# Issuing each bulk load of a row-sum kernel as two 64-partition DMAs from two queues

## The chip, the cores and the metric

The kernel runs on one core of one Trainium2 chip. The metric is the device time in microseconds (us) of one execution; medians of several runs are quoted, and lower is better. With one core, "slow" only marks a run that is over 1.5% above the fastest of the same kernel.

## The reference

The reference sums rows of 1024 numbers and divides by 1024. The input is 32 x 512 = 16384 rows, 67.1 MB in all; the output is 64 KB.

```python
def reference(x, divisor):           # x: (32, 512, 1024) float32, divisor = 1024.0
    return (np.sum(x, axis=-1) / divisor).astype(np.float32)
```

Every byte is read once, and there is next to nothing to compute. The kernel can be no faster than its loads.

## The kernel before

The 16384 rows are laid out as 128 partitions x 128 rows, so each partition owns 512 KB of consecutive memory. The loads take 8 rows of every partition at a time (4.19 MB in one DMA), all from SyncE's queue, into five tile buffers. VectorE sums five of the eight rows, ScalarE the other three.

```python
    bulk = [8] * 15
    tail = [4, 2, 1]
    pool = ctx.enter_context(tc.tile_pool(name="bulk", bufs=5))
    ...
    def sums(t, j, rows, for_act):
        d = rows - for_act
        if d:
            nc.vector.reduce_sum(out=res[:, j : j + d], in_=t[:, :d, :], axis=AX)
        for r in range(d, rows):
            act_sum(res[:, j + r : j + r + 1], t[:, r, :])

    j = 0
    for rows in bulk:
        t = pool.tile([P, 8, D], F32, name="t")
        nc.sync.dma_start(out=t[:, :rows, :], in_=xr[:, j : j + rows, :])
        sums(t, j, rows, rows * 3 // 8)
        j += rows
    ...  # loads of 4, 2 and 1 rows, and a last row in three pieces, all 128 partitions wide
```

## Time and profile before

| | before |
|---|---|
| median time | 164.75 us |
| load queues | one, 96.5% of the 16 DMA engines' span |
| rate of the loads, 40 to 120 us | 433 GB/s |
| one row of a load (32 KB in one partition) | 1.213 us, 27.0 GB/s per DMA engine |
| VectorE, ScalarE busy | 53%, 36% |

The rows of the loads are the DMA packets that the trace records, each with its size and duration; the profile page counts 3169 packets. 16 engines at 27.0 GB/s are 432 GB/s, which is the measured rate. The durations of rows were read from these records; no line of a page shows a single row. The records do not say which engine carried a row, so what the expectations below say of single engines is the author's picture and not a reading.

Three lines of the page of the kernel before. The first two cut the span into 40 slices (busy share of the DMA engines in tenths, then GB/s); the third is the load queue with its packets, MB and share of the 16 engines' time.

```profile
DMA  6999999999999999999999999999999999999990
GB/s 209 426 418 443 435 435 435 418 443 435 410 459 426 402 467 435 394 459 435 426 443 418 435 437 418 443 435 410 443 443 402 459 443 410 443 435 398 408 352 16
q1 hardware_dynamic: 3168, 67.18, 96.5%
```

The same kernel's stretches: the columns are the stretch, its length, busy time of VectorE, ScalarE and GpSimd (with instruction counts), clock, DMA share and GB/s.

```profile
40.00:80.00 40.00, 21.95 (x4) 13.79 (x24) 0.00 (x0) 1.00 1.01 433
80.00:120.00 40.00, 21.95 (x4) 13.78 (x24) 0.00 (x0) 1.00 1.01 433
```

The DMA engines do not pause from the second slice to the last landing at 158.7 us, and the two compute engines have slack. So whatever a change does to the rate of the loads, or to keeping their queue filled, shows in full in the time; what it does to the sums matters only after the last load has landed.

### The profile page before, as it was taken

To read this page: it belongs to the slowest core of one execution; us is meant where nothing else is said; L and a number is where in the kernel's file an instruction comes from. 1 tells how busy PE (TensorE), PEld (TensorE's weight loads), DVE (VectorE), ACT (ScalarE), POOL (GpSimd) and SP (SyncE) were. 2 spreads that over 40 slices of the span, in tenths; PEclk is the share of its full clock that TensorE was granted. 3 is DMA by queue.
4 is the path that set the end of the run, shared out by engine and by line. 5 is a ranking of instruction groups with operands and counts; after the bars stand their busy time and mean duration, and the time that the engine had idled before them with its cause. 6 is when DMAs were issued, how large, how long until landed. Compare 5 with 4: busy or idle time off the path is not lost.

```text
span 162.9 us, 222 instructions
## 1 busy us (share of the span) xinstructions
DVE 87.1 (53%) x22; ACT 58.1 (36%) x101; POOL 0.2 (0%) x4
## 2 busy tenths in 40 slices
DVE  0007639094571917549093672908448092763983
ACT  3006135080531607034080622608043070613692
POOL 0000000000000000000000000000000000000000
DMA  6999999999999999999999999999999999999990
GB/s 209 426 418 443 435 435 435 418 443 435 410 459 426 402 467 435 394 459 435 426 443 418 435 437 418 443 435 410 443 443 402 459 443 410 443 435 398 408 352 16
DMA packets 3169, 67.18 MB, mean 412 GB/s; under 512 B 352, under 2 KB 736, under 8 KB 992
## 3 DMA queue, kind: packets, MB, share of 16 engines
q1 hardware_dynamic: 3168, 67.18, 96.5%
q14 instruction: 1, 0.01, 0.0%
HBM read 67.11 MB, written 0.07 MB: 412 GB/s over the span
## 4 chain that ended last, share of the span: by engine, by line
DMA 90%; DVE 7%; issue 1%; SPq 0%; DVEq 0%
DMA t<-in_x_dram 61%; DMA last<-in_x_dram 30%; DVE res L53 7%; DVE part L77 0%; DVE res L76 0%; DVE part L78 0%; DVE res L79 0%; SPq L60 0%; DVE part L74 0%; DVEq L78 0%
## 5 line engine op out<-in xcount | busy, mean ns | idle before, releaser
L53 DVE TENSOR_REDUCE res<-t 128x5 f32<-128x5120 f32 x15 | 82.3, 5488 | 72.5 <-DMA t<-in_x_dram 72.5
L48 ACT ACTIVATE junk<-t 128x1024 f32<-128x1024 f32 x45 | 46.2, 1027 | 99.2 <-DMA t<-in_x_dram 98.3
L48 ACT ACTIVATION_READ_ACCUMULATOR junk<-t 128x1 f32 x45 | 8.4, 186 | 0.0
L48 ACT ACTIVATE junk<-tail 128x1024 f32<-128x1024 f32 x4 | 4.1, 1028 | 1.7 <-DMA tail<-in_x_dram 1.7
L53 DVE TENSOR_REDUCE res<-tail 128x2 f32<-128x2048 f32 (+1 forms) x2 | 3.4, 1743 | 0.0
L48 ACT ACT_TABLE_LOAD x1 | 1.3, 1283 | 0.7 <-PEq L97 0.7
L74 DVE TENSOR_REDUCE part<-last 128x1 f32<-128x512 f32 x1 | 0.7, 685 | 0.6 <-DMA last<-in_x_dram 0.6
L48 ACT ACTIVATION_READ_ACCUMULATOR junk<-tail 128x1 f32 x4 | 0.7, 186 | 0.0
L77 DVE TENSOR_REDUCE part<-last 128x1 f32<-128x256 f32 x1 | 0.4, 411 | 0.0
L48 ACT ACTIVATE junk<-last 128x256 f32<-128x256 f32 x1 | 0.4, 388 | 0.0
L76 DVE TENSOR_SCALAR res<-res 128x127 f32<-128x127 f32 x1 | 0.2, 216 | 0.0
L78 DVE TENSOR_REDUCE part<-part 128x1 f32<-128x3 f32 x1 | 0.2, 155 | 0.1
L48 ACT ACTIVATION_READ_ACCUMULATOR junk<-last 128x1 f32 x1 | 0.2, 187 | 0.0
L79 DVE TENSOR_SCALAR res<-part 128x1 f32<-128x1 f32 x1 | 0.2, 154 | 0.0
L97 POOL MEMSET const-uint8-127<- 128x1 uint8 x1 | 0.1, 102 | 0.0
L97 POOL MEMSET const-bfloat16-1.0<- 128x1 bf16 x1 | 0.1, 101 | 0.0
L97 POOL MEMSET const-float32-0.0<- 128x1 f32 x1 | 0.1, 98 | 0.2 <-issue 0.2
L97 POOL MEMSET const-float32-1.0<- 128x1 f32 x1 | 0.1, 98 | 0.0
## 6 DMA issues: line engine op xcount, KB each, us to landing
t<-in_x_dram SPq DMA_DIRECT2D x15, 4096.0 KB, 43.0
tail<-in_x_dram SPq DMA_DIRECT2D x1, 2048.0 KB, 47.5
tail<-in_x_dram SPq DMA_DIRECT2D x1, 1024.0 KB, 49.5
tail<-in_x_dram SPq DMA_DIRECT2D x1, 512.0 KB, 50.4
last<-in_x_dram SPq DMA_DIRECT2D x1, 256.0 KB, 48.2
last<-in_x_dram SPq DMA_DIRECT2D x2, 128.0 KB, 34.1
out_dram<-res SPq DMA_DIRECT2D x1, 64.0 KB, 1.5
```

The lines of the kernel that those rows point to most:

```text
L48: nc.scalar.activation(junk[:, :n], src, COPY, accum_out=dst)
L53: nc.vector.reduce_sum(out=res[:, j : j + d], in_=t[:, :d, :], axis=AX)
L74: nc.vector.reduce_sum(out=part[:, 0:1], in_=last[:, 0:h], axis=AX)
L76: nc.vector.tensor_scalar_mul(out=res[:, :j], in0=res[:, :j], scalar1=scale)
L77: nc.vector.reduce_sum(out=part[:, 2:3], in_=last[:, h + q : D], axis=AX)
L78: nc.vector.reduce_sum(out=part[:, 3:4], in_=part[:, 0:3], axis=AX)
L79: nc.vector.tensor_scalar_mul(out=res[:, j : j + 1], in0=part[:, 3:4], scalar1=scale)
L97: nc = _bacc.Bacc("TRN2", target_bir_lowering=False, num_devices=1)
```

## The change

The intent: fewer, larger loads (14 rows instead of 8), the last rows shared between VectorE and ScalarE, and each bulk load issued as two DMAs of 64 partitions, one from SyncE's queue and one from ScalarE's. The core of the diff:

```diff
-    bulk = [8] * 15
-    tail = [4, 2, 1]
-    assert sum(bulk) + sum(tail) + 1 == J
-    pool = ctx.enter_context(tc.tile_pool(name="bulk", bufs=5))
+    bulk = [14] * 8 + [8]
+    split = {14: 6, 8: 4, 4: 2, 2: 1}
+    tail = [4, 2]
+    assert sum(bulk) + sum(tail) + 2 == J
+    pool = ctx.enter_context(tc.tile_pool(name="bulk", bufs=3))
...  (four junk tiles instead of one for ScalarE's sums; ScalarE's sums stand first)
-    for rows in bulk:
-        t = pool.tile([P, 8, D], F32, name="t")
-        nc.sync.dma_start(out=t[:, :rows, :], in_=xr[:, j : j + rows, :])
-        sums(t, j, rows, rows * 3 // 8)
+    for i, rows in enumerate(bulk):
+        t = pool.tile([P, 14, D], F32, name="t")
+        for q, a in ((nc.sync, 0), (nc.scalar, P // 2)):
+            tc.keep_in_program_order(q.dma_start(out=t[a : a + P // 2, :rows, :], in_=xr[a : a + P // 2, j : j + rows, :]))
+        sums(t, j, rows)
         j += rows
...  (the last two rows are split between the engines at column 704)
```

More of the change, by code (lines that the diff above doesn't have):

```diff
@@ L33 @@
     out_v = out.tensor.reshape((P, J)).ap()
-    bulk = [8] * 15
-    tail = [4, 2, 1]
-    assert sum(bulk) + sum(tail) + 1 == J
-    pool = ctx.enter_context(tc.tile_pool(name="bulk", bufs=5))
+    bulk = [14] * 8 + [8]
[3 more added lines that the diff above has]
+    pool = ctx.enter_context(tc.tile_pool(name="bulk", bufs=3))
     one = ctx.enter_context(tc.tile_pool(name="one", bufs=1))
-    psum = ctx.enter_context(tc.tile_pool(name="junk", bufs=1, space=bass.MemoryType.PSUM))
+    psum = ctx.enter_context(tc.tile_pool(name="junk", bufs=4, space=bass.MemoryType.PSUM))
@@ L42, with sums @@
     res = one.tile([P, J], F32, name="res")
     part = one.tile([P, 4], F32, name="part")
-    junk = psum.tile([P, D], F32, name="junk")
     def act_sum(dst, src):
         n = src.shape[-1]
+        junk = psum.tile([P, D], F32, name="junk")
         nc.scalar.activation(junk[:, :n], src, COPY, accum_out=dst)
-    def sums(t, j, rows, for_act):
-        d = rows - for_act
-        if d:
-            nc.vector.reduce_sum(out=res[:, j : j + d], in_=t[:, :d, :], axis=AX)
+    def sums(t, j, rows):
+        d = rows - split[rows]
@@ L54, in sums @@
         for r in range(d, rows):
             act_sum(res[:, j + r : j + r + 1], t[:, r, :])
+        nc.vector.reduce_sum(out=res[:, j : j + d], in_=t[:, :d, :], axis=AX)
     j = 0
-    for rows in bulk:
-        t = pool.tile([P, 8, D], F32, name="t")
-        nc.sync.dma_start(out=t[:, :rows, :], in_=xr[:, j : j + rows, :])
-        sums(t, j, rows, rows * 3 // 8)
+    for i, rows in enumerate(bulk):
[3 more added lines that the diff above has]
+        sums(t, j, rows)
@@ L62 @@
         j += rows
-    for k, rows in enumerate(tail):
-        t = one.tile([P, rows, D], F32, name=f"tail{k}")
-        nc.sync.dma_start(out=t, in_=xr[:, j : j + rows, :])
-        sums(t, j, rows, (rows + 1) // 2)
+    for i, rows in enumerate(tail):
+        t = one.tile([P, rows, D], F32, name=f"tail{i}")
+        tc.keep_in_program_order(nc.sync.dma_start(out=t, in_=xr[:, j : j + rows, :]))
+        sums(t, j, rows)
         j += rows
-    h, q = D // 2, D // 4
-    last = one.tile([P, D], F32, name="last")
@@ L72 @@
-    for a, b in ((0, h), (h, h + q), (h + q, D)):
-        nc.sync.dma_start(out=last[:, a:b], in_=xr[:, j, a:b])
-    nc.vector.reduce_sum(out=part[:, 0:1], in_=last[:, 0:h], axis=AX)
-    act_sum(part[:, 1:2], last[:, h : h + q])
-    nc.vector.tensor_scalar_mul(out=res[:, :j], in0=res[:, :j], scalar1=scale)
-    nc.vector.reduce_sum(out=part[:, 2:3], in_=last[:, h + q : D], axis=AX)
-    nc.vector.reduce_sum(out=part[:, 3:4], in_=part[:, 0:3], axis=AX)
-    nc.vector.tensor_scalar_mul(out=res[:, j : j + 1], in0=part[:, 3:4], scalar1=scale)
@@ L80 @@
-    nc.sync.dma_start(out=out_v, in_=res)
+    c = 704
+    t = one.tile([P, D], F32, name="row")
+    tc.keep_in_program_order(nc.sync.dma_start(out=t, in_=xr[:, j, :]))
+    act_sum(part[:, 0:1], t[:, c:])
+    nc.vector.reduce_sum(out=part[:, 1:2], in_=t[:, :c], axis=AX)
+    nc.vector.tensor_scalar(
+        out=res[:, j : j + 1], in0=part[:, 1:2], scalar1=part[:, 0:1], scalar2=scale, op0=ADD, op1=MULT
+    )
+    nc.vector.tensor_scalar_mul(out=res[:, :j], in0=res[:, :j], scalar1=scale)
+    j += 1
@@ new lines @@
+    t = one.tile([P, D], F32, name="last")
+    tc.keep_in_program_order(nc.sync.dma_start(out=t[:, :c], in_=xr[:, j, :c]))
+    tc.keep_in_program_order(nc.sync.dma_start(out=t[:, c:], in_=xr[:, j, c:]))
+    act_sum(part[:, 2:3], t[:, :c])
+    nc.vector.reduce_sum(out=part[:, 3:4], in_=t[:, c:], axis=AX)
+    nc.vector.tensor_scalar(
+        out=res[:, j : j + 1], in0=part[:, 3:4], scalar1=part[:, 2:3], scalar2=scale, op0=ADD, op1=MULT
+    )
+    tc.keep_in_program_order(nc.sync.dma_start(out=out_v, in_=res))
```

## The prediction

> What bounds the kernel now: the loads. The page gives the one load queue 96.5% of the 16 engines' span and 412 GB/s on average; the stretches from 10 to 150 us show 429 to 433 GB/s. VectorE is busy 53%, ScalarE 36%. The chain of waits is 90% DMA; only about 2 us of compute follow the last landing (158.7 us). All loads are issued by SyncE, which does nothing else, with up to five 8-row tiles ahead, so the queue never runs dry.
>
> What the change moves. Every bulk load becomes two 64-partition halves. SyncE's halves still run ahead, three tiles deep. ScalarE's half sits in ScalarE's program: its instruction order is half of load 0, table load and six row sums of load 0, then half of load 1, six sums, half of load 2, and so on. So ScalarE's half of load k+1 starts only after load k has landed and ScalarE has summed it; only one is ever in flight. Two costs follow.
>
> 1. A serial chain per 14-row load: landing, six sums at 1.18 us (start to start in the timeline: 13.38, 14.56, 15.74), 7.1 us; issue and start[...], about 2 to 3 us (the first load took 12.63 us where 4.19 MB at 433 GB/s are 9.7 us); then the transfer of the half, 3.67 MB. VectorE's 8-row sum, 8.8 us (5.49 us for five rows), then frees the buffer for SyncE's half of load k+3, so SyncE too is held back after the first loads and its half runs beside ScalarE's, not in the gap.
>
> 2. The rate. [...]Nothing in the trace of before shows a half-width load. If the two queues overlap perfectly, a half takes 17 us (3.67 MB at half of 433) and the chain's period is about 26 us[...].
>
> Summing nine loads by such a model: about 238 us with perfect overlap[...].[...]
>
> Smaller terms: the table load (1.28 us) now waits for ScalarE's first half; SyncE's queue has no work at the end, so the last two ScalarE halves run alone; VectorE's order has the tail and last-row sums before loads 7 and 8, which costs little because ScalarE ends last. The gain meant (fewer loads, shared last rows) is under 2 us and is lost, since the last rows land long before the end.
>
> Predicted: 300 us, 8 in 10 between 225 and 345. Faster by over 2%: 1%; within 2%: 1%; slower: 98%.
>
> What would show it: two load queues on the page; GB/s in the slices falling to 200 to 300 with regular dips to about 0 to 220 while ScalarE sums; ScalarE's half issued right after the sixth sum of the load before; the chain of waits alternating ScalarE sums and DMA; SyncE waiting for buffers (for VectorE or ScalarE).[...] VectorE's and ScalarE's sums should cost the same per row.
>
> What would make it wrong: half-width loads at full rate (then about 218 us); ScalarE's issues running ahead of its sums, so that the rate alone counts (165 us with perfect overlap)[...].

The sum over nine loads had three branches: about 238 us with perfect overlap (30%), 270 to 295 us between (25%), and 336 us if the two queues' transfers did not overlap, which it called "serialized" (40%). The 300 us lie between them. Only the 238 us can be followed from the trace of the kernel before: nine loads of about 26 us each, the author's estimate from six sums at 1.18 us, 2 to 3 us of issue and start, and 17 us for 3.67 MB at half of 433 GB/s.

## The result, and the profile after

The changed kernel took 334.39 us in the median (332.5 to 335.47), against 164.75 us. The ratio is 2.03, with a 95% interval of 2.02 to 2.04. Ratios here are the mean time of one kernel's fast runs over that of the other's of the same rounds, so not quite the ratio of the medians.

The same lines of the page of the changed kernel; q1 is SyncE's queue, q10 ScalarE's.

```profile
DMA  9999989999999989899999898999999899979900
GB/s 221 221 221 214 193 165 200 221 221 221 221 221 221 221 186 186 179 221 221 221 221 221 186 221 165 201 221 221 221 221 221 173 189 260 270 156 315 198 0 8
q1 hardware_dynamic: 1584, 35.72, 49.3%
q10 hardware_dynamic: 720, 31.46, 45.0%
```

Two of the changed kernel's stretches, with the columns as before:

```profile
56.00:86.00 30.00, 0.00 (x0) 0.00 (x0) 0.00 (x0) 1.00 1.02 214
98.00:110.00 12.00, 0.00 (x0) 0.00 (x0) 0.00 (x0) 1.00 1.03 220
```

The DMA engines are as busy as before (94.3% for both queues together), but they move half as much (202 GB/s on average by the page, against 412): busy engines are not fast engines. The trace's packet records say it directly. A row of a bulk load is now 56 KB, and its median duration is 4.33 us, 13.2 GB/s per engine, where 27 GB/s would make it 2.12 us. The 62.9 MB of bulk loads at 212 GB/s (16 engines at 13.2) take 297 us; that is the time of this kernel but for the tail's 4.2 MB, the sums at the end and some gaps.

The start of the chain of waits in order of time (start, length, what):

```profile
0.73 42.23 DMA t<-in_x_dram
42.95 0.02 issue
42.98 2.23 ACT junk L50 x5
45.20 41.52 DMA t<-in_x_dram
86.73 0.02 issue
86.75 0.04 ACTq L50
86.79 0.04 issue
86.83 2.23 ACT junk L50 x5
89.06 41.41 DMA t<-in_x_dram
```

And the instructions around the first of those sums, from the timeline:

```profile
42.98 1.03 ACT L50 ACTIVATE junk<-t 128x1024 f32<-128x1024 f32 x1 [7.45 <-DMA t<-in_x_dram]
44.03 1.01 ACT L50 ACTIVATE junk<-t 128x1024 f32<-128x1024 f32 x1
45.07 1.00 ACT L50 ACTIVATE junk<-t 128x1024 f32<-128x1024 f32 x1
45.20 0.47 ACTq L62 DMA_DIRECT2D t<-in_x_dram  x1
```

ScalarE issues its next half 2.2 us after the load before has landed, while it runs its third sum: its sequencer runs ahead of its sums, although the DMA (issued at 45.20 us) stands in the program after the sixth (which starts at 48.19 us). So the chain alternates between a short ScalarE piece and some 41 us of DMA.

How the two queues share the engines is in the packet records too. Counting the rows in progress at some moments of the trace of the changed kernel (the clock is that of the views; both queues have work in all of them):

```
us         96.0    97.5    99.0    100.5   102.0   103.5   105.0   106.5
q1 rows    16      16      4       0       0       16      16      14
q10 rows   0       0       12      16      16      0       0       2
```

At 96.0 and 97.5 us all 16 rows in progress are SyncE's, at 100.5 and 102.0 us all are ScalarE's, and at 103.5 us all are SyncE's again: in this trace the two queues take turns, a row of 56 KB (4.33 us in the median) at a time. From 56 to 220 us rows into both halves of the partitions are in progress only around a change of turn, for 1.4 us each time; from 221 to 239 us two rows of one half mostly run beside 14 of the other (65% of that time), and the rows started in it take 4.26 to 4.33 us as well.

### The profile page after: what moved, and what is told of

Its sections match the earlier page's. It is cut to its first block, busy times and chain, and to the rows that moved or that the text cites. A ratio compares the mean times of both kernels' runs of the same rounds, so it can differ in the third digit from the quotient of the medians.

```text
span 332.8 us, 236 instructions
## 1 busy us (share of the span) xinstructions
DVE 78.7 (24%) x16; ACT 60.6 (18%) x115; POOL 0.2 (0%) x4
## 4 chain that ended last, share of the span: by engine, by line
DMA 64%; issue 21%; DVE 8%; ACT 5%; SPq 0%; DVEq 0%; ACTq 0%
DMA t<-in_x_dram 49%; DMA tail<-in_x_dram 15%; DVE res L56 8%; ACT junk L50 5%; DVE part L76 0%; SPq L62 0%; DVE part L88 0%; DVE res L80 0%; DVEq L123 0%; DVE res L89 0%; ACTq L50 0%; DVEq L80 0%; DVEq L56 0%
## 5 line engine op out<-in xcount | busy, mean ns | idle before, releaser
L56 DVE TENSOR_REDUCE res<-t 128x8 f32<-128x8192 f32 (+1 forms) x9 | 73.8, 8208 | 201.4 <-DMA t<-in_x_dram 201.4
L50 ACT ACTIVATE junk<-t 128x1024 f32<-128x1024 f32 x52 | 52.4, 1008 | 232.7 <-DMA t<-in_x_dram 161.3
L50 ACT ACTIVATION_READ_ACCUMULATOR junk<-t 128x1 f32 x52 | 9.7, 186 | 0.0
L50 ACT ACTIVATE junk<-tail 128x1024 f32<-128x1024 f32 x3 | 3.0, 1005 | 0.0
L76 DVE TENSOR_REDUCE part<-row 128x1 f32<-128x704 f32 x1 | 0.9, 875 | 0.0
L50 ACT ACTIVATE junk<-last 128x704 f32<-128x704 f32 x1 | 0.7, 737 | 0.0
```

The lines of the kernel that those rows point to most:

```text
L50: nc.scalar.activation(junk[:, :n], src, COPY, accum_out=dst)
L76: nc.vector.reduce_sum(out=part[:, 1:2], in_=t[:, :c], axis=AX)
```

## The experiments

Four theories at first. A: a half-width load moves at half rate, whichever queue issues it. B: ScalarE's late issue costs the time. C: two queues disturb each other. D: the 56 KB rows or the large tiles are slow.

### 1. The same loads put back together

```diff
-        for q, a in ((nc.sync, 0), (nc.scalar, P // 2)):
-            tc.keep_in_program_order(q.dma_start(out=t[a : a + P // 2, :rows, :], in_=xr[a : a + P // 2, j : j + rows, :]))
+        tc.keep_in_program_order(nc.sync.dma_start(out=t[:, :rows, :], in_=xr[:, j : j + rows, :]))
```

Expected: 

> The changed kernel with each bulk load put back together: one 128-partition load of 14 rows from SyncE. Theory A (a half-width load moves at half rate, whichever queue issues it) and theories B (ScalarE's late issue) and C (two queues disturb each other) all expect 162 to 166 us, 56 KB rows of about 2.12 us at 27 GB/s per engine. Theory D (rows of 56 KB, or 14-row tiles, are themselves slow) expects over 250 us and rows of about 4.3 us.

Measured: 164.15 us (163.99 to 164.63), ratio 0.9968 with a 95% interval of [0.9956, 0.9981] to the kernel before. Rows of 56 KB took 2.116 us. Its page, the two rate lines and the queue:

```profile
DMA  6999999999999999999999999999999998999990
GB/s 226 452 452 452 438 410 424 424 438 396 410 452 452 453 452 452 438 424 410 424 438 396 410 455 452 453 452 452 438 396 424 424 452 378 428 444 388 408 371 21
q1 hardware_dynamic: 2160, 67.18, 96.4%
```

Theory D falls. The rest of the change (14-row loads, three buffers, shared last rows) is worth 0.3%, and all of the loss, 170 us, belongs to splitting the loads. This version is also the only one that beat both kernels, by that 0.3%.

### 2. Both halves from SyncE

```diff
-        for q, a in ((nc.sync, 0), (nc.scalar, P // 2)):
+        for q, a in ((nc.sync, 0), (nc.sync, P // 2)):
```

Expected: 

> Both 64-partition halves issued by SyncE, none by ScalarE. Theory A: 305 to 320 us (63 MB at 212 GB/s are 297 us, 4.2 MB at 430 are 10 us, a few us of start and end), rows still 4.3 us, one load queue. Theories B and C: 163 to 175 us, since neither ScalarE's program nor a second queue is left.

Measured: 321.85 us (321.74 to 322.01); one load queue; rows of 4.48 us. Its page:

```profile
q1 hardware_dynamic: 2304, 67.18, 98.3%
```

Theory A missed by 2 us above its range (its rows were to take 4.3 us, not 4.48), and B and C missed by about 150 us: neither a second queue nor ScalarE's program is needed for the loss. Against the changed kernel, 12.5 us are left for those two.

### 3. Two queues, whole width

```diff
-        for q, a in ((nc.sync, 0), (nc.scalar, P // 2)):
-            tc.keep_in_program_order(q.dma_start(out=t[a : a + P // 2, :rows, :], in_=xr[a : a + P // 2, j : j + rows, :]))
+        half = rows // 2
+        for q, a in ((nc.sync, 0), (nc.scalar, half)):
+            tc.keep_in_program_order(q.dma_start(out=t[:, a : a + half, :], in_=xr[:, j + a : j + a + half, :]))
```

Expected: 

> Two queues as in the change, ScalarE's DMAs at the same places in its program, but each DMA holds 7 rows of all 128 partitions. Theory A: 163 to 175 us, rows of 28 KB at about 27 GB/s per engine, a few us lost where ScalarE's late issue lets the queues run dry. Theory B: about 230 us or more (a period of some 26 us per load). Theory C: over 250 us, with rows at about half rate while both queues have work.

Measured: 177.27 us in the median (fast runs 176.89 to 177.39, and one of 180.89, marked slow, which is the profiled one), ratio 1.075 [1.074, 1.077]. Rows of 28 KB took 1.062 us in the median in both queues, 27 GB/s. Theory C falls: two queues with whole-width loads run at full rate. What remains of B is real but small: 13 us over the one-queue version, 2 us above the upper end that I had expected. Part of it is ScalarE's late issue: the engines run nearly dry at 124 to 126 us and at 158.5 to 161 us, each time until ScalarE has issued its next half (124.90 and 160.46 us), and the slices of the page fall there. The other part is the end: from 167.5 us until the output leaves at 177.6 us no load is left, against 2.2 us in experiment 1.

```profile
GB/s 211 423 448 423 442 416 423 455 423 435 423 455 416 435 429 384 391 435 416 416 416 448 435 335 384 410 448 301 320 423 417 428 471 402 403 180 359 110 0 15
```

### 4. ScalarE's halves issued ahead

The program first issues loads 0 to 2, then load k+3 after the sums of load k:

```diff
+    for i in range(3):
+        load(i)                        # the same two half-width DMAs, from the same two queues
+    for i, rows in enumerate(bulk):
+        sums(tiles[i], starts[i], rows)
+        if i + 3 < len(bulk):
+            load(i + 3)
```

Expected: 

> The change, but ScalarE issues its halves of loads 0, 1 and 2 first, and load k+3 after the sums of load k: both queues always have work. Theory A with engines in step: 300 to 318 us, only the idle time between loads and the late sums are saved, rows still 4.3 us. Theory B: 163 to 180 us, since its halves are no longer late.[...]

Measured: 314.52 us (313.64 to 315.96), ratio 1.91; rows of 4.27 us. Its page has both queues at 98.3% together:

```profile
q1 hardware_dynamic: 1584, 35.72, 50.9%
q10 hardware_dynamic: 720, 31.46, 47.4%
```

With both queues filled, the rate rises by 5% over experiment 2 (rows of 4.27 us, not 4.48) and no more, so two halves in flight at once do not add up. This is what "engines in step" expected. The kernel is 20 us faster than the changed one, but not by the earlier issue alone: here a tail load lands last, and the tail's sums also come after those of the bulk loads in VectorE's order. In the two profiled runs the last load landed 10 us earlier, and the time from there until the output left fell from 13.7 to 2.2 us.

### 5. The middle 64 partitions

So far the 64 partitions were always 0 to 63 or 64 to 127. This run asks whether the choice of the 64 counts: 32 to 95 in one load, the outer quarters apart. The reason that the expectation gave for its first branch is cut, as no run shows it; its times stand: 2.15 us a row into 32 to 95 and 4.3 us into the outer partitions.

```diff
-        for q, a in ((nc.sync, 0), (nc.scalar, P // 2)):
-            tc.keep_in_program_order(q.dma_start(out=t[a : a + P // 2, :rows, :], in_=xr[a : a + P // 2, j : j + rows, :]))
+        for q, a, b in ((nc.sync, 32, 96), (nc.sync, 0, 32), (nc.sync, 96, 128)):
+            tc.keep_in_program_order(q.dma_start(out=t[a:b, :rows, :], in_=xr[a:b, j : j + rows, :]))
```

Expected: 

> All loads from SyncE's queue; each bulk load is three DMAs: partitions 32 to 95 (64 partitions), then 0 to 31, then 96 to 127.[...] their 56 KB rows take about 2.15 us, and the other two DMAs' rows 4.3 us: 63 MB half at 433 and half at 212 GB/s, 72 + 149 + 10 us and ends, 230 to 255 us. If any DMA of 64 or fewer partitions is slow as such: all rows 4.3 us, 305 to 320 us.

Measured: 272.21 us in the median, with a wide spread (262.83, the only run not marked slow, to 278.24); that is 17 us over the range, and 8 us over it in the fast run. In the first load of the profiled run, after the start, the rows into 32 to 95 took 2.12 us (a few up to 2.4) and the rows into the outer partitions 3.8 to 4.5 us. So half-width as such is not slow (2.12 us, where 0 to 63 and 64 to 127 took 4.48 us in experiment 2); which half counts. Later in the run loads of both kinds overlap, with rows from 2.1 to 7.2 us; less of the time is fast than I had summed, and the runs did not settle why.

### 6. The same, with other memory behind the middle partitions

So far the partitions written and the part of the input read changed together. Here partitions 32 to 95 get the first half of the input, and 0 to 31 the third quarter; the output is written back to match.

```diff
+        for a, b, s in ((32, 96, 0), (0, 32, 64), (96, 128, 96)):
+            tc.keep_in_program_order(nc.sync.dma_start(out=t[a:b, :rows, :], in_=xr[s : s + b - a, j : j + rows, :]))
```

Expected: 

> As the kernel with partitions 32 to 95 as one load, but that load now reads the blocks of x that partitions 0 to 63 had (the first half of x), 0 to 31 get the third quarter; the output is written back in the matching order, so the result stays right. If the slow rate belongs to the SBUF side (partitions written): the load into 32 to 95 runs at 2.12 us a row, the other two at 4.3, in all 260 to 280 us as before the swap. If it belongs to the HBM side (which part of x the engines read at once): its rows take 4.3 us, all rows do, 305 to 325 us.

Measured: 270.01 us in the median, again wide (248.44, the only run not marked slow and below the range, to 279.38). The first load's rows into 32 to 95 took 2.12 us after the start, although they now came from the memory that was slow into 0 to 63 (4.48 us in experiment 2), and those into the outer partitions 3.8 to 4.5 us. The rate belongs to the partitions written, not to the memory read.

### 7. Even and odd partitions, one queue

```diff
-        for q, a in ((nc.sync, 0), (nc.scalar, P // 2)):
-            tc.keep_in_program_order(q.dma_start(out=t[a : a + P // 2, :rows, :], in_=xr[a : a + P // 2, j : j + rows, :]))
+        for q, a in ((nc.sync, 0), (nc.sync, 1)):
+            tc.keep_in_program_order(q.dma_start(out=t[a:P:2, :rows, :], in_=xr[a:P:2, j : j + rows, :]))
```

Expected: 

> All loads from SyncE's queue; each bulk load is two DMAs of 64 partitions: the even ones, then the odd ones.[...] about 165 us.[...] rows of about 4.3 us and 300 to 320 us.

Measured: 164.59 us (164.4 to 164.72), ratio 0.9992 [0.9977, 1.0007]; rows of 2.116 us.

```profile
GB/s 225 408 422 422 422 436 394 450 422 450 450 450 450 450 422 408 408 436 408 436 436 450 422 453 450 450 450 422 408 422 422 408 436 424 426 434 390 416 370 23
q1 hardware_dynamic: 2304, 67.18, 96.3%
```

The branch of 300 us or more falls, and the one of 165 us holds. What the run shows is that the even 64 partitions and the odd 64 both move at the pace of whole-width loads, 2.116 us a row.

### 8. Even and odd partitions, two queues

The change itself, with only the choice of the 64 partitions different:

```diff
-        for q, a in ((nc.sync, 0), (nc.scalar, P // 2)):
-            tc.keep_in_program_order(q.dma_start(out=t[a : a + P // 2, :rows, :], in_=xr[a : a + P // 2, j : j + rows, :]))
+        for q, a in ((nc.sync, 0), (nc.scalar, 1)):
+            tc.keep_in_program_order(q.dma_start(out=t[a:P:2, :rows, :], in_=xr[a:P:2, j : j + rows, :]))
```

Expected: 

> The change with one thing different: SyncE's 64 partitions are the even ones and ScalarE's the odd ones; program, queues and sizes as in the change. If which 64 partitions is the whole loss of rate, rows of 56 KB take about 2.12 us and the time is that of two full-width queues, 170 to 185 us, the rest over 164 us being ScalarE's late issue and the tail sums that sit early in VectorE's order. If two half-width DMAs from two queues are slow whatever their partitions: over 300 us.

Measured: 184.19 us in the median (180.09, the only run not marked slow, to 185.45; the range of the expectation holds the median); rows of 2.116 us. The page of the slowest of these runs:

```profile
GB/s 200 450 450 487 400 412 400 400 437 437 475 450 400 400 437 362 387 412 462 412 475 437 400 389 412 400 412 212 487 385 400 494 401 382 385 278 0 0 0 14
q1 hardware_dynamic: 1584, 35.72, 45.9%
q10 hardware_dynamic: 720, 31.46, 40.9%
```

This is the cleanest cut of all: only the choice of partitions changed, and 150 of the 170 us are gone (154 by the fast run). What is left over 164 us lies before and after the last landing. In this profiled run the last load landed at 165.8 us, 7 us later than in experiment 1, and 16.4 us passed from there until the output left, against 2.2 us there; so some 14 of the 21 us lie after the last landing. What landed last was ScalarE's half of the eight-row load, with 9 us of sums still to do on ScalarE and 15 us on VectorE. The end reads so in its timeline, where the sums of a bulk load (128x8) wait behind those of the tail in VectorE's order:

```profile
154.59 2.29 DVE L56 TENSOR_REDUCE res<-tail 128x2 f32<-128x2048 f32 x1 [23.77 <-DMA tail<-in_x_dram]
156.79 8.68 DVE L56 TENSOR_REDUCE res<-t 128x8 f32<-128x8192 f32 x1
167.70 13.00 DVE L56 TENSOR_REDUCE res<-t 128x8 f32<-128x8192 f32 x2
```

VectorE waited 23.8 us for a tail load, although a bulk load had landed by 137.7 us, when ScalarE began to sum it; and it ended 6 us after ScalarE (ScalarE's last sum ended at 174.7, VectorE's last bulk sum at 180.7). No run changed that order alone.

### 9 to 11. Putting the engines out of step

In the counts of rows in progress above, all 16 rows were of one queue's half most of the time (73% of 56 to 250 us). If being in step is what costs the rate, a nudge that lets some engines carry rows of one half while the others carry rows of the other should give fast rows. The nudge is a tiny load in SyncE's queue ahead of its first half. That it would put as many engines out of step as it has partitions was the assumption; the rows in progress, below, show what each load did. To the kernel of experiment 4:

```diff
+    tail0 = one.tile([P, 4, D], F32, name="tail0")
+    nc.vector.memset(tail0[0:8, 0:2, :], 0.0)      # SyncE starts about 2 us late
+    tc.keep_in_program_order(nc.sync.dma_start(out=tail0[0:8, 0, 0:512], in_=xr[0:8, 0, 0:512]))
```

Expected of 8 partitions: 

> The kernel with ScalarE's halves issued ahead, plus one load of 8 partitions x 2 KB (16 KB in all[...]) put in front of SyncE's first half; SyncE starts about 2 us late, behind a memset, so that ScalarE's rows come first.[...] If engines in step are the cause, rows drop from 4.3 to about 2.2 us while both queues have work, and a packet-by-packet estimate from the measured 27 GB/s per engine gives 205 to 250 us (the phase is lost again late). If two queues serialize for another reason: unchanged against the kernel without the wedge, 300 to 320 us.

Measured: 317.65 us (317.1 to 318.37). The nudge itself worked: from 25 to 27 us of the trace, eight rows of each queue were in progress. But the shortest of the 1024 rows of 56 KB took 3.58 us; the median was 4.36.

Expected of a single number: 

> As the wedge kernel, but the extra load in front of SyncE's first half is a single number[...]. If engines slow each other in fixed pairs[...]: exactly two of 16 engines run their rows at about 2.15 us for some loads, the other 14 at 4.3, some 50 to 130 of the 1024 rows of 56 KB fast, and the time is still 305 to 318 us. If the limit is one of the whole half of SBUF or of the queues, no row is at 2.15 us.

Expected of 4 partitions: 

> The extra load has 4 partitions[...]. With pairs: if the four engines are of four different pairs, eight engines run fast (200 to 500 of the 1024 rows near 2.15 us); if they are two whole pairs, no row is fast, as with eight engines. The time stays near 305 to 318 us, set by the slow engines.

Measured, in one run each: 315.3 and 316.08 us, and again no fast row. In the first, three of 16 engines were out of step at 12 to 15 us of the trace (13 rows of one queue and 3 of the other in progress); in the second, five. From 29 to 31.4 us of the single-number run, one row of ScalarE's queue ran beside 15 of SyncE's and still took 4.34 us, about what the 15 took (4.31 to 4.38). So the theory of fixed pairs of engines falls too, and with it my explanation by step alone: a row that was alone in its half of the partitions for more than half of its time (2.4 of 4.34 us) was no faster.

### 12. Many shapes, one at a time

With one tile buffer, each bulk load starts on idle DMA engines (the second is issued at 47.76 us, after the last sum of the first at 46.6 us). The first DMA of each load has one set of partitions; the rest of the load follows in shorter rows. The result stays correct.

```diff
+    shapes = [span(a, a + 64) for a in (0, 8, 16, 24, 32)]
+    shapes.append((slice(0, P, 8), [slice(k, P, 8) for k in range(1, 8)]))
+    shapes.append((slice(0, 64, 4), [slice(k, 64, 4) for k in range(1, 4)] + [slice(64, P)]))
+    shapes.append(span(48, 80))
+    shapes.append(span(56, 72))
...
+        first, rest = shapes[i]
+        tc.keep_in_program_order(nc.sync.dma_start(out=t[first, :rows, :], in_=xr[first, j : j + rows, :]))
```

Expected: 

> A measuring kernel, slow on purpose: one tile buffer, so every bulk load starts on idle DMA engines, all from SyncE. The first DMA of each load has rows of 14 x 4 KB and one set of partitions: 0-63, 8-71, 16-79, 24-87, 32-95, then every 8th (16 in all), every 4th of 0-63 (16), 48-79, and 56-71 (rows of 8 x 4 KB); the rest of the load follows in rows half as long. Read: how long the first rows took. Theory H (each half of SBUF, partitions 0-63 and 64-127, takes about 217 GB/s, shared by the engines that write there): 4.3 us for 0-63; for 8-71 14 rows of about 3.7 us and two of 2.1; 16-79 12 of 3.2 and four of 2.1; 24-87 ten of 2.7 and six of 2.1; 32-95, every 8th and 48-79 2.1; every 4th of 0-63 4.3; 56-71 1.2 (its shorter row).[...] Theory G (one conflict anywhere slows all engines alike): in each load all 16 first rows take the same, 4.3 or between.

Measured (one look; its time, 453 us, means nothing). The column has the second row of every engine where there is one, because the first contains the start. For comparison, rows of whole-width loads took 2.116 us for 56 KB (experiment 1) and 1.213 us for 32 KB (the kernel before).

| partitions | measured, us per row |
|---|---|
| 0-63 | 4.48 to 4.49 |
| 8-71 | 4.41 to 4.43 |
| 16-79 | 4.46 to 4.48 |
| 24-87 | 4.42 to 4.44 |
| 32-95 | 2.12 (two rows to 2.46) |
| 48-79 | 4.40 to 4.49 |
| every 8th of 128 | 3.98 to 4.91 (first rows) |
| every 4th of 0-63 | 3.27 to 4.51 (first rows) |
| 56-71, 32 KB rows | 4.81 from first start to last end |

Theory H, one limit per half of the partitions (its 217 GB/s is half of the 433 GB/s measured before the change), falls: it wanted full rate, 2.1 us, for 48 to 79 (4.40 to 4.49 us) and for every 8th partition (3.98 to 4.91 us). A further theory wanted twelve fast rows and four slow ones in 24 to 87, and all 16 took the same (4.42 to 4.44 us), so it falls as well. Theory G was right that all engines of a load go at one pace, in the six loads that have second rows (within 0.01 to 0.09 us of each other, but for two rows of 32 to 95).

What tells a fast set from a slow one was not shown. The measured sets rule out two simple answers. It is not the number of partitions: 64 took 2.12 us (32 to 95) and 4.42 to 4.44 us (24 to 87, eight lower), and every 8th, only 16, took 3.98 us or more (first rows; the start made the first rows of the kernel before at most 0.9 us longer, 2.11 us instead of 1.21). It is not enough to have as many partitions below 64 as above: 32 to 95 has, and so have 48 to 79 and every 8th, which were slow. Nor do the runs show why two slow loads in two queues do not overlap, not even with the engines out of step (4.36 us a row in the median of experiment 9).

## Why the prediction was right

**What bounds the kernel: right.** It named the rate of the loads and their queue; the changed kernel's DMA engines are still 94% busy, and its time is its bytes over a halved rate.

**The rate, the deciding term: right in kind, and the worst case came true, though nothing had shown it.** The trace of the kernel before held no half-width load, so the rates that the branches assumed were not measured here. The runs show these for 0 to 63 and 64 to 127: 16 engines at the measured row make 205 GB/s with one queue (4.48 us, experiment 2) and 212 to 215 GB/s with two (4.33 and 4.27 us), 5% more at most. The branch "serialized", 336 us, met the 334.4 us, and that it met it to 2 us is partly luck: it assumed a higher rate than the 212 GB/s measured (35 us for the 7.34 MB of a load) and a longer chain than the measured one (below), and the two errors offset. The 300 us was the middle of a hedge between that branch (40%) and two gentler ones.

**The chain through ScalarE: right in direction, mis-sized.** The term "six sums at 1.18 us, 7.1 us" before ScalarE's next half measured 2.2 us, because its issue runs ahead of its sums and these took 1.04 us each, start to start (42.98, 44.03, 45.07). "ScalarE's half issued right after the sixth sum" is wrong; it came during the third. And the chain hardly sets the time: SyncE's halves fill the engines meanwhile. Issuing ahead gained 20 us of 170 (experiment 4), and more than half of that at the end. That SyncE would wait for buffers was right: before its bulk loads the trace puts down 142.6 us of waiting to VectorE's sums and 105.5 us to landings.

**"Regular dips to about 0 to 220": only half right.** There are dips to between 156 and 200 GB/s, but the DMA engines stop for no more than 0.3 us in all before the last landing.

**The end: partly wrong.** The prediction said that VectorE's order "costs little because ScalarE ends last"; but VectorE ended last, by 2.2 us (329.8 against 327.6). After the last bulk load had landed (ScalarE's sums of it began at 318.98 us), VectorE still had 11 us of sums that stood behind the tail's.

```profile
305.91 8.68 DVE L56 TENSOR_REDUCE res<-t 128x8 f32<-128x8192 f32 x1
316.81 13.00 DVE L56 TENSOR_REDUCE res<-t 128x8 f32<-128x8192 f32 x2
```

**The gain meant: right.** It is 0.3% when the loads are whole (experiment 1), and is lost here.

So the 170 us divide, by experiments 1, 2 and 8, as follows. Which partitions a load covers: about 150 us (334.4 to 184.2 when only that is changed, 154 by the one fast run) to 158 us (164.15 to 321.85). The second queue, with its late issue and the order at the end: 12 to 20 us; no run changed the late issue and that order separately.

## What to carry to other kernels

Before splitting a load by partitions, measure the rows of the split load. Here 64 partitions at full rate (2.12 us a row of 56 KB: 32 to 95, the even ones, the odd ones) and 64 at half rate (4.48 us: 0 to 63, 64 to 127) differ only in which ones they are; which other sets are fast, these runs do not tell. If a split is wanted at all, the two that kept the full rate here were by rows (1.062 us for 28 KB) and in even and odd partitions (2.116 us for 56 KB). A second queue added no rate here to whole-width loads (27 GB/s per engine with one and with two) and 5% to half-width ones (4.27 us a row, not 4.48). In the changed kernel ScalarE's next half was issued only 2.2 us after the landing of the load before; with what it changed at the end, the second queue cost 13 us here even with whole-width loads. Read the busy share of the DMA engines together with GB/s or with the duration of a packet: 94% busy was 202 GB/s here, where 96.5% busy had been 412.
